# The key stage of an RWKV-7 layer in fp32: PE order by hand, head sums on quarters of the array, on-chip low-rank results, stores from ACT

## The chip, the cores and the metric

The kernel runs on one core of a Trainium2 chip. The metric is the device time of one launch in microseconds: the median of three runs. Engines are called PE (TensorE, matrix products; PEld is its weight load), DVE (VectorE), ACT (ScalarE), POOL (GpSimd) and SP (SyncE, which here only issues transfers). Each engine takes its own instructions strictly in order and waits on semaphores for the others.

## The reference

A decoder trunk with two layers over 272 tokens (16 learned tokens and 256 of the input) of 2048 features: an RWKV-7 time mixing, a gated linear attention, each followed by a squared-ReLU MLP. The change lies in the time mixing of the first layer. What matters of it:

```python
def rwkv7_time_mix(x, v_first, mix, w_rkv, w0, w1, w2, a0, a1, a2, g1, g2, k_k, k_a, r_k,
                   ln_w, ln_b, w_o, vres):
    xx = jnp.pad(x, ((0, 0), (1, 0), (0, 0)))[:, :-1] - x
    xr, xw, xk, xv, xa, xg = (x + xx * mix[i] for i in range(6))
    r = xr @ w_rkv[0]
    k = xk @ w_rkv[1]
    v = xv @ w_rkv[2]
...
    w_log = -jax.nn.softplus(-(w0 + jnp.tanh(xw @ w1) @ w2)) - 0.5
    a = jax.nn.sigmoid(a0 + (xa @ a1) @ a2)
    kk = hs(k * k_k)
    kk = kk / jnp.maximum(jnp.sqrt(jnp.sum(kk * kk, axis=-1, keepdims=True)), 1e-12)
    k = k * (1.0 + (a - 1.0) * k_a)
    decay = jnp.exp(-jnp.exp(hs(w_log)))
    y = rwkv7_scan(rh, decay, kh, vh, -kk, kk * ah)
...
    bonus = (jnp.sum(rh * kh * r_k, axis=-1, keepdims=True) * vh).reshape(B, T, D)
```

`hs` splits the 2048 features into 32 heads of 64. The scan is computed in chunks of 64 tokens: the products of decayed keys and queries, a triangular system for each head that is inverted, and a state step for each chunk.

## The kernel before

Features lie on the 128 partitions, tokens along the free dimension, so a tensor of the layer is 16 tiles of 128 x 272. A weight for one output tile comes in two halves of 512 KB. `wload` (line 128) loads a half with SP into `raw` (three buffers), ACT rounds it into `hi` (line 140), DVE subtracts into `lo` (line 141), both with two buffers; the PE then does 24 matmuls on it (`mm3`, lines 163 to 165: hi by x-high, hi by x-low, lo by x-high). A tile of a projection is thus 48 matmuls of 128 x 128 by 272.

The key stage (lines 567 to 618) runs over the 16 tiles f of the key projection. In each:

- `proj` gives k in a PSUM bank (`pj`, or `pry` for every third tile).
- `ca` holds the decay's cumulated sum and `a` of this tile. The low-rank function `lora` (lines 470 to 481) made them during the stage before, for all 16 tiles, and stored them to DRAM as `cad`; here they are loaded again. ACT turns the first into `W` and `iW` (L574, L575), one buffer for `W` and two for `iW`.
- ACT makes `kk` (L576), its square `sq` (L577) and `kn` (L578). The sum of `sq` within each head is a matmul of the full array with `bones`, a matrix of ones in two 64 x 64 blocks on the diagonal (L580). ACT makes an inverse root of it (L581, L582), DVE scales `kk` (L584).
- DVE fills two tiles of 128 x 576 with `put`: `bk` (the keys, L300 with `iW`) and `ar` (kk and r with `W`). Both have two buffers. SP stores them to DRAM as `bkd` and `ard` (L590, L593).
- DVE makes r times k times r_k in `kn` (L591), a second full matmul with `bones` sums it (L595), ACT copies that over `r` (L596).

Into the same loop are put: at f = 0 the blend of the value projection's input, `mix(3)`; at f = 7 the transfers that fetch the first eight tiles' `bk` and `ar` in another layout, 1 MB each (`fetch`, into `BK0` and `AR0`); at f = 10 to 13 the products of keys and queries (`scores`, PE L525, DVE `AM`); from f = 13 the steps of the inversion (`invert`, all on DVE). The value projection follows at once.

Each engine's order comes from a scheduler that follows the order of the program and moves instructions ahead where it reckons that they fit, with weight loads and casts at a higher priority; the order is fixed when the kernel is built. It puts a sum of tile f between two matmuls of tile f + 1. Only in the later part of the layer is the PE's order written out by hand (`tc.manual_schedule`).

Of the kernel before, what the change touches and what calls it, by code (L numbers as in the profile page):

```python
# [11 lines left out]
F32R = mybir.dt.float32r  # L12
AF = mybir.ActivationFunctionType
ALU = mybir.AluOpType
# [40 lines left out]
class Kern:  # L55
# [242 lines left out]
    def rwkv(self, done):  # L298
# [171 lines left out]
        def lora(f):  # L470
            l2 = self.t(e2, [96, 2, P], "l2", 3)
            nc.sync.dma_start(l2, ap["lora2"][f])
            st = self.t(ep, [P, 2, T], "ca", 2)
# [7 lines left out]
            nc.sync.dma_start(cad[f], st.rearrange("p a t -> p (a t)"))  # L481

        xg = mix32(5, ep)
        for f in range(NR + 2, KT):
            nc.scalar.copy(self.two(rr[f]), self.proj(pair(wr, f), xr, T))
            if f == NR + 2:
                for i in range(2):
                    nc.scalar.activation(gs[i], self.proj32(pair(lw, 2 + i), xg, T), AF.Sigmoid)
                xk = mix(2, ep)
            for i in range(3 if f < 14 else 2):  # L490
                lora(3 * (f - 10) + i if f < 14 else 12 + 2 * (f - 14) + i)
# [4 lines left out]
        Wf = self.t(ep, [P, T + 1], "W")  # L496
        nc.gpsimd.memset(Wf[:, 0:1], 1.0)
        W = Wf[:, 1:]
# [68 lines left out]
        for f in range(KT):  # L567
            r = rr[f]
            bk, ar = st2[0][f % 2], st2[1][f % 2]
            ps = self.proj(pair(wk, f), xk, T, bank=self.pry if f % 3 == 2 else None)  # L570
            ca = self.t(ep, [P, 2, T], "ca", 2)
            nc.sync.dma_start(ca.rearrange("p a t -> p (a t)"), cad[f])
            iW, kk, sq, kn = (self.t(ep, [P, T], n, 2) for n in ("iW", "kk", "sq", "kn"))
            nc.scalar.activation(W, ca[:, 0], AF.Exp, scale=-DECAY)  # L574
            nc.scalar.activation(iW, ca[:, 0], AF.Exp, scale=DECAY)  # L575
            nc.scalar.mul(self.two(kk), ps, self.vec("k_k", f))  # L576
            nc.scalar.activation(sq, kk, AF.Square)  # L577
            nc.scalar.activation(kn, ca[:, 1], AF.Identity, scale=self.vec("k_a", f), bias=self.omka[:, f : f + 1])  # L578
            ss = self.pm()[:, :T]
            nc.tensor.matmul(ss, self.bones, sq, start=True, stop=True)  # L580
# [3 lines left out]
            nc.vector.scalar_tensor_tensor(out=kk, in0=sq, scalar=1e12, in1=kk, op0=ALU.min, op1=ALU.mult)  # L584
            put(ar, 0, kk, Wf[:, :T], 1)
            nc.vector.tensor_copy(ar[:, 0:513:128], kk[:, ::C])
# [4 lines left out]
            nc.vector.scalar_tensor_tensor(out=kn, in0=r, scalar=self.vec("r_k", f), in1=kn, op0=ALU.mult, op1=ALU.mult)  # L591
            put(ar, 1, r, W)
            nc.sync.dma_start(ard[f], ar)  # L593
            rk = self.pu()[:, :T]
            nc.tensor.matmul(rk, self.bones, kn, start=True, stop=True)  # L595
            nc.scalar.copy(r, rk)  # L596
            nc.vector.tensor_copy(WC[:, f], W[:, C - 1 : 4 * C : C])
            if f == 0:
                xv = mix(3, self.xp)
                early2.close()  # L600
                wl = ExitStack()
                lp = wl.enter_context(tc.tile_pool(name="wl", bufs=1, reuse_waits="tile"))
                BKs, ARs = ([self.t(lp, [P, 8, 256], n)] for n in ("BK0", "AR0"))
                AMs, AMrs = [self.t(lp, [P, 2, 16, 128], "AM0")], []
                sysA = self.t(lp, [P, 32, 32], "sysA")
                t11 = sysA.rearrange("p a b -> p (a b)")[64:96].rearrange("p (c h s) -> p c h s", c=2, h=16)
                nc.gpsimd.memset(sysA, 0.0)
# [14 lines left out]
        BKs.append(self.t(kp, [P, 8, 320], "BK1"))  # L622
# [699 lines left out]
```

## Time and profile before

| | us |
|---|---|
| median of 3 runs | 2402.7 (2400.86 to 2403.1) |
| the profiled execution | 2402.54 |
| its span in the profile | 2400.8 |
| the key stage, 155.31 to 278.90 | 123.59 |

A row of the PE's timeline has the start in us, the duration in us, engine, line and operation, the tile written and the tiles read, the shapes and a count; a bracket at the end gives the idle time before it and who ended that. One fp32 matmul by `bones` leaves two records (x2), a fast one leaves one. In a group's row the two numbers after the bar are busy us and mean ns of one, and behind the second bar stands idle time before them.

### The profile page before, as it was taken

The page shows a single profiled execution, that of the slowest core. Times are in us where ns is not written, and L with a number is a line of the kernel's source. Part 1 is how long each engine was busy: PE and PEld are TensorE (multiplying, and loading weights), DVE is VectorE, ACT ScalarE, POOL GpSimd, SP SyncE. Part 2 cuts the span into 40 slices and gives each one's busy share as a digit, 9 for nine tenths or more (in the row PEclk, how much of TensorE's full clock was granted, in tenths as well). Part 3 has the DMA queues.
Part 4 walks back from the last instruction along what each step waited for, and adds up shares of the span by engine and source line. Part 5 has one row for each costly group of instructions (what it writes and reads, how often), then busy time and mean ns, then how long its engine had stood idle before and what let it go on. Part 6 is the DMA issues. An engine that isn't in the chain of part 4 may idle for free. (4 is left out here: it accounts for less than half of the span.)

```text
span 2400.8 us, 48047 instructions
## 1 busy us (share of the span) xinstructions
PE 2360.9 (98%) x19689; PEld 2244.1 (93%) x19689; DVE 1611.9 (67%) x2734; ACT 1242.4 (52%) x1975; POOL 6.6 (0%) x20
## 2 busy tenths in 40 slices
PE   9999999899999999999999999999999999999998
PEld 8888888889999999999999999999999999999997
DVE  8777886858655555555556777767666666666666
ACT  6376644556555445445345556555555445445444
POOL 0000000000000000000000000000000000000000
PEclk9999999999999999999999999999999999999999
DMA  6578864524555555555555554455555555555554
GB/s 210 169 235 293 248 190 146 146 83 163 183 187 193 187 191 191 188 193 186 192 189 190 196 181 167 159 176 193 182 201 200 200 201 200 202 202 202 201 201 169
DMA packets 160732, 455.34 MB, mean 190 GB/s; under 512 B 34112, under 2 KB 50624, under 8 KB 160512
## 3 DMA queue, kind: packets, MB, share of 16 engines
q1 hardware_dynamic: 160512, 452.27, 55.8%
q8 instruction: 154, 2.52, 0.4%
q14 instruction: 66, 0.54, 0.1%
HBM read 433.86 MB, written 18.35 MB: 188 GB/s over the span
## 5 line engine op out<-in xcount | busy, mean ns | idle before, releaser
L141 DVE TENSOR_TENSOR lo<-raw,hi 128x1024 fp32r<-128x1024 f32 (+1 forms) x818 | 927.4, 1140 | 534.1 <-ACT hi L140 525.9
L140 ACT CAST hi<-raw 128x1024 fp32r<-128x1024 f32 (+1 forms) x818 | 794.6, 979 | 939.4 <-PE pj L164 546.8
L163 PE MATMUL pj<-x,hi 128*128 128x272 f32 (+1 forms) x2624 | 748.6, 285 | 1.7 <-DVE hres L300 1.0
L165 PE MATMUL pj<-x,lo 128*128 128x272 f32 (+1 forms) x2624 | 734.5, 280 | 4.3 <-DVE lo L141 4.1
L164 PE MATMUL pj<-x,hi 128*128 128x272 f32 (+1 forms) x2624 | 734.0, 280 | 0.2 <-DVE x L240 0.2
L163 PEld LDWEIGHTS pj<-x,hi 128*128 128x128 f32 x2624 | 498.1, 190 | 10.2 <-issue 3.7
L165 PEld LDWEIGHTS pj<-x,lo 128*128 128x128 f32 x2624 | 498.2, 190 | 7.2 <-DVE lo L141 6.5
L164 PEld LDWEIGHTS pj<-x,hi 128*128 128x128 f32 x2624 | 498.2, 190 | 3.6 <-issue 1.4
L196 PE MATMUL pj<-x,hi 128*128 128x512 f32 x1280 | 419.9, 382 | 0.1
L197 PE MATMUL pj<-x,lo 128*128 128x256 f32 x1280 | 348.8, 273 | 0.0
L196 PE MATMUL pj<-h,hi 128*128 128x512 f32 x1008 | 330.3, 382 | 0.0
L163 PE MATMUL pj<-h,hi 128*128 128x272 f32 (+1 forms) x1040 | 290.1, 279 | 0.0
L164 PE MATMUL pj<-h,hi 128*128 128x272 f32 (+1 forms) x1040 | 290.1, 279 | 0.0
L165 PE MATMUL pj<-h,lo 128*128 128x272 f32 (+1 forms) x1040 | 290.1, 279 | 0.0
L197 PE MATMUL pj<-h,lo 128*128 128x256 f32 x1008 | 274.8, 273 | 0.0
L196 PEld LDWEIGHTS pj<-x,hi 128*128 128x128 f32 x1280 | 241.9, 189 | 34.1 <-DVE x L996 0.4
L197 PEld LDWEIGHTS pj<-x,lo 128*128 128x128 f32 x1280 | 245.7, 192 | 0.3 <-DVE lo L141 0.2
L196 PEld LDWEIGHTS pj<-h,hi 128*128 128x128 f32 x1008 | 190.5, 189 | 26.5
L163 PEld LDWEIGHTS pj<-h,hi 128*128 128x128 f32 x1040 | 196.6, 189 | 0.0
L164 PEld LDWEIGHTS pj<-h,hi 128*128 128x128 f32 x1040 | 196.6, 189 | 0.0
L165 PEld LDWEIGHTS pj<-h,lo 128*128 128x128 f32 x1040 | 196.6, 189 | 0.0
L197 PEld LDWEIGHTS pj<-h,lo 128*128 128x128 f32 x1008 | 193.5, 192 | 0.0
(270 smaller groups left out, 2077.2 us busy)
## 6 DMA issues: line engine op xcount, KB each, us to landing
raw<-mlp_w_d SPq DMA_DIRECT2D x512, 512.0 KB, 3.3
raw<-gla_in_d SPq DMA_DIRECT2D x98, 512.0 KB, 3.2
raw<-w_rkv_d SPq DMA_DIRECT2D x80, 512.0 KB, 3.9
raw<-gla_o_d SPq DMA_DIRECT2D x32, 512.0 KB, 4.3
raw<-w_r_d SPq DMA_DIRECT2D x16, 512.0 KB, 3.3
raw<-rw_oQ_d SPq DMA_DIRECT2D x16, 512.0 KB, 3.2
ard<-ar SPq DMA_DIRECT2D x16, 288.0 KB, 3.4
bkd<-bk SPq DMA_DIRECT2D x16, 288.0 KB, 3.5
```

The costliest lines, as they stand in the source:

```text
L140: nc.scalar.copy(hi[:, h], raw[:, h])
L141: nc.vector.tensor_tensor(out=lo[:, h], in0=raw[:, h], in1=hi[:, h].bitcast(F32), op=ALU.subtract)
L163: nc.tensor.matmul(out, hi[:, ws], xh, start=first, stop=False)
L164: nc.tensor.matmul(out, hi[:, ws], xl, start=False, stop=False)
L165: nc.tensor.matmul(out, lo[:, ws], xh, start=False, stop=last)
L196: nc.tensor.matmul(wide, hi[:, ws], xt, start=kt == 0, stop=False)
L197: nc.tensor.matmul(one, lo[:, ws], xt[:, 0], start=False, stop=kt == nk - 1)
```

## The change

Nothing else in the layer is computed differently. By parts:

- The PE's order in the key stage is written out by hand: half of tile f, `sums` of tile f - 1, the other half of tile f. `rest(f - 1)` stands between the halves in the program, too, and so shifts the place of all other engines' work.
- `sums` replaces both full matmuls with `bones` by four of 64 x 64: two on the array's diagonal quarters for `sq` (into `pm`), two on the other two quarters for the tile before's `kn` (into `pu`, with the two heads swapped; ACT copies them back crosswise, L595, in two copies of 64 partitions).
- `lora` keeps the results of tiles 0 to 7 in `hres` in SBUF and stores none of them. Those of tiles 8 to 15 are stored, and each is loaded into the place that tile f - 8 has left (L637).
- `W` has two buffers. r times W and k times iW are put before the inverse root's result is used. The five-column copy into `ar` and the copy into `WC` move from DVE to ACT (L632, L639).
- The stores of `bk` and `ar` are issued by ACT. In tiles 4 to 7 each is split in two, with one part going straight into `BK0`, `AR0` or `BK1`; tiles 0 to 3 are fetched into these by SP at f = 5, 6 and 7. `BK1` (the second keys) gets a place of its own from the start of the stage, and its later fetch goes.
- The blend for the value projection is made during the stage before, in place; only its rounding (`hl`) remains, at f = 1. `scores` and the inversion begin one tile earlier.

```diff
--- before.py
+++ after.py
@@ -470,7 +470,7 @@
         def lora(f):
             l2 = self.t(e2, [96, 2, P], "l2", 3)
             nc.sync.dma_start(l2, ap["lora2"][f])
-            st = self.t(ep, [P, 2, T], "ca", 2)
+            st = hres[:, 2 * f : 2 * f + 2] if f < NR else self.t(ep, [P, 2, T], "ca", 2)
...
             nc.vector.tensor_tensor_scan(out=st[:, 0], data0=m64, data1=sg, initial=0.0, op0=ALU.mult, op1=ALU.add)
-            nc.sync.dma_start(cad[f], st.rearrange("p a t -> p (a t)"))
+            if f >= NR:
+                nc.sync.dma_start(cad[f], st.rearrange("p a t -> p (a t)"))
...
                 xk = mix(2, ep)
+            if f == KT - 2:
+                for kt in range(KT):
+                    mixed(d[:, kt], kt, 3)
             for i in range(3 if f < 14 else 2):
                 lora(3 * (f - 10) + i if f < 14 else 12 + 2 * (f - 14) + i)
         tc.keep_in_program_order(nc.scalar.preload_act_table_set("natural_log_exp_and_others"))
         st2 = [[self.t(ep, [P, 576], n, 2) for i in range(2)] for n in ("bk", "ar")]
         for x in st2[0] + st2[1]:
             nc.gpsimd.memset(x[:, 512:], 0.0)
-        Wf = self.t(ep, [P, T + 1], "W")
-        nc.gpsimd.memset(Wf[:, 0:1], 1.0)
-        W = Wf[:, 1:]
+        Wfs = [self.t(ep, [P, T + 1], "W", 2) for _ in range(2)]
+        for x in Wfs:
+            nc.gpsimd.memset(x[:, 0:1], 1.0)
 
         def put(dst, slot, a, b, skip=0):
             v = dst[:, :512].rearrange("q (c s t) -> q c s t", c=4, s=2)[:, :, slot]
@@ -564,62 +568,114 @@
                 for rows, x in reversed(blocks(c, slice(0, 16))):
                     nc.sync.dma_start(x, invd[b][rows].rearrange("h s t -> s h t"))
 
-        for f in range(KT):
-            r = rr[f]
+        def store(f, dst, x, i):
+            q = nc.scalar
+            if 3 < f < 8:
+                q.dma_start((BKs, ARs)[i][0][:, f], x[:, :256])
+                q.dma_start(dst[f][:, 256:] if i else BKs[1][:, f], x[:, 256:])
+            else:
+                q.dma_start(dst[f], x)
+
+        held, tiles = [], {}
+
+        half = lambda q: slice(HEAD * q, HEAD * q + HEAD)
+
+        def sums(sq):
+            ss, last = self.pm()[:, :T] if sq is not None else None, held.pop() if held else None
+            todo = [(sq, ss, 0)] if sq is not None else []
+            if last:
+                r, kn = last
+                rk = self.pu()[:, :T]
+                todo.append((kn, rk, 1))
+            for x, out, i in todo:
+                for q in range(2):
+                    nc.tensor.matmul(out[half(q ^ i)], self.bones[half(q), half(q)], x[half(q)], start=True, stop=True)
+            if last:
+                for q in range(2):
+                    nc.scalar.copy(r[half(q)], rk[half(1 - q)])
+            return ss
+
+        def keyproj(f, ps, half):
+            hi, lo = self.wload(pair(wk, f)[half])
+            for j in range(8):
+                kt = 8 * half + j
+                self.mm3(ps, hi, lo, slice(j * P, (j + 1) * P), xk[kt][:, 0], xk[kt][:, 1], kt == 0, kt == KT - 1)
+
+        def front(f, ps):
+            kk, sq = (self.t(ep, [P, T], n, 2) for n in ("kk", "sq"))
+            ps = self.back(ps)
+            nc.scalar.mul(self.two(kk), ps, self.vec("k_k", f))
+            nc.scalar.activation(sq, kk, AF.Square)
+            tiles[f] = ps, kk, sq
+
+        def rest(f):
+            r, Wf = rr[f], Wfs[f % 2]
+            W = Wf[:, 1:]
             bk, ar = st2[0][f % 2], st2[1][f % 2]
-            ps = self.proj(pair(wk, f), xk, T, bank=self.pry if f % 3 == 2 else None)
-            ca = self.t(ep, [P, 2, T], "ca", 2)
-            nc.sync.dma_start(ca.rearrange("p a t -> p (a t)"), cad[f])
-            iW, kk, sq, kn = (self.t(ep, [P, T], n, 2) for n in ("iW", "kk", "sq", "kn"))
+            ps, kk, sq = tiles.pop(f)
+            i = f % NR
+            ca = hres[:, 2 * i : 2 * i + 2]
+            iW, kn = (self.t(ep, [P, T], n, 2) for n in ("iW", "kn"))
+            nc.scalar.activation(kn, ca[:, 1], AF.Identity, scale=self.vec("k_a", f), bias=self.omka[:, f : f + 1])
+            tt(self.two(kn), ps, self.two(kn))
+            ss = sums(sq)
             nc.scalar.activation(W, ca[:, 0], AF.Exp, scale=-DECAY)
             nc.scalar.activation(iW, ca[:, 0], AF.Exp, scale=DECAY)
-            nc.scalar.mul(self.two(kk), ps, self.vec("k_k", f))
-            nc.scalar.activation(sq, kk, AF.Square)
-            nc.scalar.activation(kn, ca[:, 1], AF.Identity, scale=self.vec("k_a", f), bias=self.omka[:, f : f + 1])
-            ss = self.pm()[:, :T]
-            nc.tensor.matmul(ss, self.bones, sq, start=True, stop=True)
             nc.scalar.activation(sq, ss, AF.Ln, bias=self.tiny)
             nc.scalar.activation(sq, sq, AF.Exp, scale=-0.5)
-            tt(self.two(kn), ps, self.two(kn))
+            put(bk, 0, kn, iW)
+            put(ar, 1, r, W)
+            nc.vector.scalar_tensor_tensor(out=kn, in0=r, scalar=self.vec("r_k", f), in1=kn, op0=ALU.mult, op1=ALU.mult)
+            held.append((r, kn))
             nc.vector.scalar_tensor_tensor(out=kk, in0=sq, scalar=1e12, in1=kk, op0=ALU.min, op1=ALU.mult)
             put(ar, 0, kk, Wf[:, :T], 1)
-            nc.vector.tensor_copy(ar[:, 0:513:128], kk[:, ::C])
+            nc.scalar.copy(ar[:, 0:513:128], kk[:, ::C])
+            store(f, ard, ar, 1)
             tt(kk, kk, ca[:, 1])
             put(bk, 1, kk, iW)
-            put(bk, 0, kn, iW)
-            nc.sync.dma_start(bkd[f], bk)
-            nc.vector.scalar_tensor_tensor(out=kn, in0=r, scalar=self.vec("r_k", f), in1=kn, op0=ALU.mult, op1=ALU.mult)
-            put(ar, 1, r, W)
-            nc.sync.dma_start(ard[f], ar)
-            rk = self.pu()[:, :T]
-            nc.tensor.matmul(rk, self.bones, kn, start=True, stop=True)
-            nc.scalar.copy(r, rk)
-            nc.vector.tensor_copy(WC[:, f], W[:, C - 1 : 4 * C : C])
-            if f == 0:
-                xv = mix(3, self.xp)
...
-            if f == 7:
-                fetch(0, BKs, bkd)
-                fetch(0, ARs, ard)
-            if 9 < f < 14:
-                scores(0, (f - 10) // 2, f % 2)
-            if f == 13:
-                inv = invert(0)
-            if f > 13:
-                for _ in range(6):
-                    next(inv, None)
+            if f < NR:
+                nc.sync.dma_start(ca.rearrange("p a t -> p (a t)"), cad[f + NR])
+            store(f, bkd, bk, 0)
+            nc.scalar.copy(WC[:, f], W[:, C - 1 : 4 * C : C])
+
+        with tc.manual_schedule(engines={ENG.PE}):
+            for f in range(KT + 1):
+                if f < KT:
+                    ps = (self.pry if f % 3 == 2 else self.pj)()[:, :T]
+                    keyproj(f, ps, 0)
+                if f:
+                    rest(f - 1)
+                if f < KT:
+                    keyproj(f, ps, 1)
+                    front(f, ps)
+                if f == 1:
+                    xv = [self.t(self.xp, [P, 2, T], "x", KT, F32R) for _ in range(KT)]
+                    for kt in range(KT):
+                        hl(xv[kt], d[:, kt])
...
+                    BKs.append(self.t(lp, [P, 8, 320], "BK1"))
...
+                if f in (5, 6, 7):
+                    dst, src, i, j = ((BKs[0], bkd, 0, 256), (ARs[0], ard, 0, 256), (BKs[1], bkd, 256, 576))[f - 5]
+                    nc.sync.dma_start(dst[:, :4], src[:4, :, i:j].rearrange("f p n -> p f n"))
+                if 8 < f < 13:
+                    scores(0, (f - 9) // 2, (f + 1) % 2)
+                if f == 12:
+                    inv = invert(0)
+                if f > 12:
+                    for _ in range(6):
+                        next(inv, None)
+            sums(None)
...
-        BKs.append(self.t(kp, [P, 8, 320], "BK1"))
@@ -892,7 +948,6 @@
         units1 = ((2, 0), (2, 1), (3, 0), (3, 1), (4, 0))
         self.split_parts = 2
         for i in ((0, 128), (128, 320)):
-            fetch(1, BKs, bkd, i)
             fetch(1, ARs, ard, i)
         ahead()
         with tc.manual_schedule(engines={mybir.EngineType.PE}):
```

Three places where the instructions' order differs. In the rows, a name's number tells buffers apart, and `waits` names the engine, or the DMA queue (DMAHW), whose semaphore the instruction waits for; a wait on its own engine guards a result still on its way.

DVE, up to a tile's `kk`. 1790 and 1791 are the two buffers of `ar`, `bk` likewise; `r_23` is r of tile 8, `r_24` and `r_25` are those of tiles 9 and 10. Before, tile 8 (the first row follows the `kk` of tile 7):

```order
L300 TENSOR_TENSOR ar_1790<-r_23_97,W_1796 128x4x64 [waits DMAHW7_49,Activation_49]
L300 TENSOR_TENSOR bk_1789<-kk_2616,iW_2615 128x4x64 [waits DVE_49]
L300 TENSOR_TENSOR bk_1789<-kk_2616,iW_2615 128x16
L300 TENSOR_TENSOR ar_1790<-r_23_97,W_1796 128x16
L597 COPY WC_105<-W_1796 128x4
L141 TENSOR_TENSOR lo_2778<-raw_2775,hi_2777 128x1024 [waits DMAHW0_49,PE_49,Activation_49]
L300 TENSOR_TENSOR kn_2715<-pry_2649,kn_2715 128x272 [waits Activation_49]
L300 TENSOR_TENSOR bk_1788<-kn_2715,iW_2712 128x4x64 [waits DMAHW1_49,DVE_49]
L300 TENSOR_TENSOR bk_1788<-kn_2715,iW_2712 128x16
L591 SCALAR_TENSOR_TENSOR kn_2715<-r_23_97,vecs_126,kn_2715 128x272 [waits DVE_49]
L584 SCALAR_TENSOR_TENSOR kk_2713<-sq_2714,kk_2713 128x272 [waits Activation_49]
L300 TENSOR_TENSOR ar_1790<-kk_2713,W_1796 128x4x64 [waits DVE_49]
```

After, from behind the `kk` of tile 8 to that of tile 9:

```order
L300 TENSOR_TENSOR kn_2849<-pj_2707,kn_2849 128x272 [waits Activation_49]
L300 TENSOR_TENSOR ar_1790<-r_25_99,W_1796 128x4x64 [waits DMAHW3_49]
L300 TENSOR_TENSOR bk_1789<-kn_2849,iW_2848 128x4x64 [waits DMAHW7_49,DMAHW0_49,DVE_49]
L300 TENSOR_TENSOR bk_1789<-kn_2849,iW_2848 128x16
L300 TENSOR_TENSOR ar_1790<-r_25_99,W_1796 128x16
L628 SCALAR_TENSOR_TENSOR kn_2849<-r_24_98,vecs_126,kn_2849 128x272 [waits DVE_49]
L141 TENSOR_TENSOR lo_2931<-raw_2928,hi_2930 128x1024 [waits DMAHW1_49,PE_49,Activation_49]
L630 SCALAR_TENSOR_TENSOR kk_2799<-sq_2800,kk_2799 128x272 [waits Activation_49]
L300 TENSOR_TENSOR ar_1791<-kk_2799,W_1797 128x4x64 [waits DVE_49]
L300 TENSOR_TENSOR ar_1791<-kk_2799,W_1797 128x15
```

The product of r and W for a tile (`ar<-r`) used to stand behind the `kk` of the tile before, and so a whole tile after the buffer's last store was issued. Now the product of tile 10 stands ahead of the `kk` of tile 9, behind that of tile 8, and waits for the DMA that stores tile 8's `ar` from the same buffer.

ACT, at a tile's `kk` and `sq`, where the next weight cast (`hi`) stands. Before:

```order
L140 CAST hi_2300<-raw_2298 128x1024 [waits DMAHW6_49,PE_49]
L575 ACTIVATE iW_2235<-ca_2233 128x272
L576 ACTIVATE kk_2236<-pj_2172,vecs_126 128x272 [waits PE_49]
L578 ACTIVATE kn_2238<-ca_2233,om_k_a_206,vecs_126 128x272
L577 ACTIVATE sq_2237<-kk_2236 128x272 [waits Activation_49]
L140 CAST hi_2365<-raw_2363 128x1024 [waits DMAHW0_49,PE_49]
L581 ACTIVATE sq_2237<-pm_2244,tiny_128 128x272 [waits PE_49]
L582 ACTIVATE sq_2237<-sq_2237 128x272 [waits Activation_49]
```

After (tile 1):

```order
L632 COPY ar_1790<-kk_1863 128x5 [waits DVE_49,Pool_49]
L622 ACTIVATE W_1796<-hres_72 128x272 [waits DVE_49]
L577 DMA ard_80<-ar_1790 128x576 [waits Activation_49]
L140 CAST hi_2082<-raw_2080 128x1024 [waits DMAHW5_49,PE_49]
L577 DMA bkd_79<-bk_1788 128x576 [waits DVE_49]
L607 ACTIVATE kk_1955<-pj_1867,vecs_126 128x272 [waits PE_49]
L140 CAST hi_2117<-raw_2115 128x1024 [waits DMAHW6_49,PE_49]
L608 ACTIVATE sq_1956<-kk_1955 128x272 [waits Activation_49]
L623 ACTIVATE iW_2145<-hres_72 128x272
L639 COPY WC_105<-W_1796 128x4
L624 ACTIVATE sq_1956<-pm_2052,tiny_128 128x272 [waits PE_49,Activation_49]
```

Here the cast, which waits for the PE to free a weight buffer, has moved between `kk` and `sq`; the logarithm of the summed `sq` (L624) stands behind it. The order is of this kind in tiles 1, 3, 5, 7 and 13, and `sq` stands ahead of the cast in the others. The store of `ar` follows the five-column copy, the store of `bk` follows the cast before.

PE, at a sum. Before:

```order
L163 MATMUL pj_2457<-x_1209,hi_2460 128x272
L164 MATMUL pj_2457<-x_1209,hi_2460 128x272
L165 MATMUL pj_2457<-x_1209,lo_2461 128x272
L580 MATMUL pm_2434<-sq_2427,cst_125 128x272 [waits Activation_49]
L163 MATMUL pj_2457<-x_1210,hi_2460 128x272
L164 MATMUL pj_2457<-x_1210,hi_2460 128x272
L165 MATMUL pj_2457<-x_1210,lo_2461 128x272
```

After:

```order
L163 MATMUL pj_2508<-x_1212,hi_2511 128x272
L164 MATMUL pj_2508<-x_1212,hi_2511 128x272
L165 MATMUL pj_2508<-x_1212,lo_2512 128x272
L592 MATMUL pm_2543<-sq_2504,cst_125 64x272 [waits PE_49,Activation_49]
L592 MATMUL pm_2543<-sq_2504,cst_125 64x272
L592 MATMUL pu_2544<-kn_2440,cst_125 64x272 [waits DVE_49]
L592 MATMUL pu_2544<-kn_2440,cst_125 64x272
L163 MATMUL pj_2508<-x_1213,hi_2575 128x272
L164 MATMUL pj_2508<-x_1213,hi_2575 128x272
```

Single sums that stood within a half, one for `sq` and, elsewhere in the tile, one for `kn`, have become one group of four between two halves.

More of the change, by code (lines that the diff above doesn't have):

```diff
@@ L597, in rwkv @@
-            nc.vector.tensor_copy(WC[:, f], W[:, C - 1 : 4 * C : C])
-            if f == 0:
-                xv = mix(3, self.xp)
[L600 to L607, printed above, removed]
@@ new lines, in rwkv @@
+        with tc.manual_schedule(engines={ENG.PE}):
[12 more added lines that the diff above has]
+                        hl(xv[kt], d[:, kt])
+                    early2.close()
+                    wl = ExitStack()
+                    lp = wl.enter_context(tc.tile_pool(name="wl", bufs=1, reuse_waits="tile"))
+                    BKs, ARs = ([self.t(lp, [P, 8, 256], n)] for n in ("BK0", "AR0"))
+                    BKs.append(self.t(lp, [P, 8, 320], "BK1"))
+                    AMs, AMrs = [self.t(lp, [P, 2, 16, 128], "AM0")], []
+                    sysA = self.t(lp, [P, 32, 32], "sysA")
+                    t11 = sysA.rearrange("p a b -> p (a b)")[64:96].rearrange("p (c h s) -> p c h s", c=2, h=16)
+                    nc.gpsimd.memset(sysA, 0.0)
+                if f in (5, 6, 7):
[9 more added lines that the diff above has]
+            sums(None)
```

## The prediction

> **What bounds the kernel now.** I read the page's first parts and the chain of waits, then the windows of the key stage, then the PE's timeline and waits inside it. TensorE is busy 98% of the span at full clock, and the chain that ended last holds no engine but PE.
>
> ```profile
> PE 2360.9 (98%) x19689; PEld 2244.1 (93%) x19689; DVE 1611.9 (67%) x2734; ACT 1242.4 (52%) x1975; POOL 6.6 (0%) x20
> ...
> PEclk9999999999999999999999999999999999999999
> ...
> PE 28%; DVE 0%; ACT 0%; DVEq 0%; issue 0%
> 155.31:278.90 123.59, 117.08 (x900) 108.71 (x899) 105.29 (x275) 86.41 (x170) 1.11 (x2) 1.00 0.82 267
> 278.90:301.47 22.57, 20.82 (x172) 20.14 (x171) 21.32 (x62) 11.79 (x26) 0.00 (x0) 1.00 0.81 265
> ```
>
> The two window rows (length; then PE, PEld, DVE, ACT, POOL; clock, DMA share, GB/s) are the key stage, from its first matmul to its last, and the start of the v-projection. In the key stage the PE is still the fullest engine (117 of 123.6 us), but DVE has 105, ACT 86, and the DMA engines are 82% busy. What can be won is PE's extra work and its waits; what can be lost is a wait on any of the others.
>
> ```profile
> 154.59 0.62 PE L475 MATMUL pm<-tw,l 96*128 96x272 f32 x2
> 155.05 0.62 PE L476 MATMUL pry<-ta,l 96*128 96x272 f32 x2
> ...
> 201.04 0.72 PE L580 MATMUL pm<-sq,cst 128*128 128x272 f32 x2
> ...
> 201.72 0.28 PE L164 MATMUL pj<-x,hi 128*128 128x272 f32 x1
> ...
> 207.62 0.28 PE L165 MATMUL pj<-x,lo 128*128 128x272 f32 x1
> 208.03 0.73 PE L580 MATMUL pm<-sq,cst 128*128 128x272 f32 x2
> ...
> 288.26 0.28 PE L164 MATMUL pj<-x,hi 128*128 128x272 f32 x1
> ...
> 301.24 0.28 PE L165 MATMUL pj<-x,lo 128*128 128x272 f32 x1
> PE pm L580 <- ACT sq L577: 3.8, 5, 1.7
> PE pu L595 <- DVE kn L591: 2.0, 3, 1.7
> PE pt L525 <- DMA BK<-bkd: 1.4, 1, 1.4
> ```
>
> One tile is the time between two `L580`: 208.03 − 201.04 = 7.0 us. From 288.26 to 301.24 the PE runs 113 fast matmuls in a row, 112 steps of 0.116 us, so the 48 of a tile take 5.55. The low-rank pair shows one fp32 matmul at full size: 155.05 − 154.59 = 0.46 us (its two records are its two passes). From 201.72 to 207.62 there are 46 fast steps (5.33) and one `L595`, so an inserted sum costs 0.57: 0.46 and 0.11 of changing over. Two of them, and a wait of about 0.3 for `sq`, make up the 7.0. The three waits rows (155 to 300 us; total, times, longest) hold 7.2 us in all.
>
> **The change, part by part.** *PE order and sums.* A tile becomes 24 matmuls, four quarter matmuls, 24 matmuls. If all four quarters run at once they take 0.57 with the changeover, if two by two 2 × 0.46 + 0.11 = 1.03, if one by one 4 × 0.46 + 0.11 = 1.95. The nearest rows are the 64×64 matmuls of the state steps:
>
> ```profile
> L720 PE MATMUL pry<-AR,S 64*64 64x64 f32 x32 | 1.6, 231 | 0.0
> L722 PE MATMUL pu<-S,AR 64*64 64x64 f32 x32 | 1.2, 221 | 0.0
> 353.75 0.27 PE L722 MATMUL pu<-S,AR 64*64 64x64 f32 x1
> ```
>
> Their 64 records begin at 353.75 and end within the window's 355.2, about 1.45 us. One by one a record of 64 columns would take 0.46 / 2 × 64 / 272 = 0.054, together 3.46 us. So 2.4 ran at once, pipeline fill included. I take 0.75 and keep 0.57 and 1.95. A tile then costs the PE 5.55 + 0.75 = 6.3 us where nothing waits.
>
> The Trainium skill, page "TensorEngine Tiling (Array Packing)", section "Gotcha 1: PSUM Pressure", says that different row tiles cannot access the same PSUM bank simultaneously; both `sq` quarters write `pm` and lie in different row tiles. By it the quarters go two by two at best and the time would be 2398.2 by the sum below. The 2.4 of the state rows, whose row tiles also share a bank, speaks against a strict form of it.
>
> *ACT order.* In tiles 1, 3, 5, 7 and 13 the changed ACT order sets a weight cast, which waits for the PE to finish the half before, ahead of `sq` (the second order listing above). The cast and `sq` then delay the sums by their lengths, 1.04 + 0.43, about 1.45 us. Five such tiles: +7.25. If another wait holds the PE anyway, this hides in it.
>
> ```profile
> L140 ACT CAST hi<-raw 128x1024 fp32r<-128x1024 f32 x16 | 16.7, 1044 | 6.7 <-PE pj L164 5.0 <-PE pry L164 1.7
> L577 ACT ACTIVATE sq<-kk 128x272 f32<-128x272 f32 x8 | 3.4, 429 | 0.2
> ```
>
> *Scores.* Four inserts of `L525` as before, 1.2 us each, one tile earlier (4.8 in all); the 1.4 us wait for `BK` goes, since half of it is copied inside the chip and the rest fetched in three parts.
>
> *The ar loop.* The product `r·W` of tile f+2 now stands on DVE ahead of the `kk` of tile f+1, and must wait until the store of tile f's `ar`, two buffers back, has landed (the first order listing). Before, it stood behind the `kk` of tile f+1, a whole tile after that store was issued. Queued behind it are `bk`, `kn`, a weight's `lo` part, and then tile f+1's own `kk`, whose store the next round waits for. So a round of DVE and DMA closes on itself, whatever PE does:
>
> ```profile
> 217.03 0.44 DVE L584 SCALAR_TENSOR_TENSOR kk<-sq,kk 128x272 f32<-128x272 f32 x1
> 217.51 0.51 DVE L300 TENSOR_TENSOR ar<-kk,W 128x256 f32<-128x256 f32 x2
> 217.97 0.17 DVE L586 COPY ar<-kk 128x5 f32<-128x5 f32 x1
> 218.07 1.23 DVE L141 TENSOR_TENSOR lo<-raw,hi 128x1024 fp32r<-128x1024 f32 x1
> 219.22 0.43 DVE L300 TENSOR_TENSOR kk<-kk,ca 128x272 f32<-128x272 f32 x1
> 219.57 0.42 DVE L300 TENSOR_TENSOR ar<-r,W 128x256 f32<-128x256 f32 x1
> 219.91 0.50 DVE L300 TENSOR_TENSOR bk<-kk,iW 128x256 f32<-128x256 f32 x2
> 220.33 0.17 DVE L300 TENSOR_TENSOR ar<-r,W 128x16 f32<-128x16 f32 x1
> 220.41 0.16 DVE L597 COPY WC<-W 128x4 f32<-128x4 f32 x1
> ...
> 223.56 0.50 DVE L591 SCALAR_TENSOR_TENSOR kn<-r,vecs,kn 128x272 f32<-128x272 f32 x1
> 224.02 0.44 DVE L584 SCALAR_TENSOR_TENSOR kk<-sq,kk 128x272 f32<-128x272 f32 x1
> DMA to landing us min/median/max: 2.2/3.4/5.5
> raw<-w_rkv_d SPq DMA_DIRECT2D x35, 512.0 KB, 4.2
> ```
>
> From start to start: `kk` 0.48, its put 0.46, the five-column copy on ACT some 0.26 with its semaphores, so the store is issued 1.2 after `kk` begins. It lands after L. Then 0.05, `ar<-r` 0.34, `bk` 0.42, the last columns 0.08, `L591` 0.46, `lo` 1.15: 2.5. A round is 3.7 + L. In tiles 0 and 2 `kn` stands inside it too (0.46 by the step 223.56 to 224.02 of an operation of that size), in tiles 1 and 3 `kn` and a second `lo` (+1.6), in tile 12 `kn` and four steps of the inversion (+1.25; a step at 0.2, an estimate from the small rows above). Tile 13 is filled with inversion steps, 7.1 by adding the same rows and sixteen steps.
>
> The trace has no DMA issued by ACT. L is bounded below by the fastest `ard` store, 2.2, and above by the loads' 4.2, which such a store could come to share; the median of the same 288 KB is 3.4. On ACT's own queue the store no longer stands behind SP's loads, and 2.2 MB of `ca` loads (of 33 MB at 267 GB/s) leave the stage. I take the middle of minimum and median, 2.8.
>
> The Trainium skill, page "DMA: Bandwidth & Descriptors", section "Issuing engines are not separate DMA queues", says that issuing from several engines saves only the issuing time, since all run on the same 16 DMA engines. By it L stays 3.4. No row of this trace can show which.
>
> *The sum of the key stage.* The first sums come 9.35 us after its start (48 + 24 matmuls 8.33, one low-rank pair 0.92, 0.1 of gaps); then 14 rounds; then 0.75 + 2.78 to its end. At L = 2.8: tiles 0 and 2 2 × 6.96, tiles 1 and 3 2 × 8.1, tiles 4 to 7 by PE (6.3 and 7.75 in turn) 28.1, tiles 8 to 11 by PE with scores 4 × 7.5, tile 12 7.75, tile 13 7.1: 103.1. End at 116.0 against 123.6 before: −7.6.
>
> *Behind it.* The sums of tile 15 already wait 1.75 us among the v-projection's matmuls:
>
> ```profile
> 281.37 0.28 PE L165 MATMUL pj<-x,lo 128*128 128x272 f32 x1
> 283.39 0.72 PE L580 MATMUL pm<-sq,cst 128*128 128x272 f32 x2 [1.75 <-ACT sq L577]
> ...
> 313.72 0.38 PE L165 MATMUL pj<-x,lo 128*128 128x272 f32 x1 [1.03 <-DVE lo L141]
> ...
> 326.33 0.38 PE L165 MATMUL pj<-x,lo 128*128 128x272 f32 x1 [1.03 <-DVE lo L141]
> ```
>
> Now ACT's `kk` of tile 15 stands behind a copy that waits for DVE, and DVE has a `lo` (1.15) in front: +1.35. The last `kn` sum, alone, adds 0.45. Quarters for full matmuls save 0.1. The two waits of 1.03 for `lo` should shrink, since inversion starts a tile earlier: −0.8. Together +0.9.
>
> *Costed at nothing.* The sixteen blends moved ahead of the stage (DVE is free a third of the span, and no PE wait above lies there; uncovered, 16 operations of the size of `L591`, 0.5 us each, would be 8 us); the copies and issues moved to ACT, below 0.5 us each by the ACT rows, hidden while ACT (86 of 123.6 us) waits for PE; without that cover they put up to 1 us a tile on the ACT order above. Fewer SP issues free a queue that bounds nothing.
>
> **Rivals.** (1) *The stores land as before*, L = 3.4: rounds 7.56, 8.7, 7.1, 7.5 (PE), 8.35, 7.1 sum to 106.4, end 119.3, −4.3 + 0.9: 2399.1. For it: same bytes, DMA 82% busy; against: the freed queue. (2) *The loop never closes*, L near 2.2 or less of a chain than I read: PE alone, 14 × 6.3 + 7.25 + 4.8 = 100.3, end 113.2, −10.4 + 0.9: 2393.0. (3) *Slower: ACT's stores share the engines evenly with the 512 KB loads* and land like them, 4.2: rounds 8.36, 9.5, 7.9, 7.9, 9.15, 7.9 sum to 116.0, end 128.9, +5.3 + 0.9: 2408.7. It decides from L = 3.75 (no gain) and passes +0.2% at 4.1. For it: 82% DMA share; four issues a tile in tiles 4 to 7. Against: 3.4 now, behind SP's loads. (4) *The quarters do not overlap*: 14 × 7.5 + 7.25 + 4.8 = 117, end 131.1: 2410.9. Against: the state rows.
>
> **How the numbers follow.** All sums stand against the profiled execution, 2402.54 us with a span of 2400.8; the median 2402.7 is the same within 0.2. Forecast: 2402.5 − 7.6 + 0.9 = 2395.8, say 2396, chance 0.35. Rivals: (1) 0.18, (2) 0.25, (3) 0.17, (4) 0.05. The likeliest one's own range, L from 2.5 to 3.1 and sums from 0.6 to 0.9, is 2394 to 2398. The 8-in-10 range must hold (1), (2) and most of (3): 2389 (case 2 with half of the ACT waits hidden) to 2408. A run here can tell 0.2%, 4.8 us, from no change. Faster by more: most of the forecast 0.29, all of (2), a little of (1): 0.58. Within: the rest of these and a part of (3): 0.23. Slower: 0.19.
>
> **What would show it.** Between the halves of a tile, from the last fast matmul to the next, about 0.75 us where nothing waits; over 1 says two by two, near 2 rival (4). Sums that wait some 1.4 us on `sq` in tiles 1, 3, 5, 7, 13. `ar<-r` on DVE held by a DMA in most tiles from 0 to 7, and `ard` landing some 2.8 us after its issue; no such idle time says rival (2), over 4 us rival (3). The key stage some 116 us long; a wait near 3.1 before tile 15's sums. The forecast is wrong if DVE's idle time there comes from ACT, not from a store, or if ACT falls behind its casts so that `lo` holds the PE.

## The result, and the profile after

| | before | changed |
|---|---|---|
| median, us | 2402.06 (2399.43 to 2405.4, 14 runs) | 2406.38 (2404.42 to 2413.38, 14 runs) |
| ratio, 95% interval | | 1.0022 (1.0015 to 1.0029) |
| profiled execution, us | 2402.54 | 2408.51 |
| its span, us | 2400.8 | 2406.7 |

The change makes the kernel slower by 0.22%. The forecast was 2396 us; the time lies inside the range of 2389 to 2408, close to rival (3), and on the other side of "before".

The page's engine row and the queue of ACT's transfers (packets, MB, share), then the two windows that answer to those shown of before (length; PE, PEld, DVE, ACT, POOL; clock, DMA share, GB/s):

```profile
PE 2355.9 (98%) x19753; PEld 2236.7 (93%) x19753; DVE 1608.9 (67%) x2702; ACT 1257.9 (52%) x2027; POOL 6.7 (0%) x21
...
q10 hardware_dynamic: 5760, 9.44, 1.1%
```

```profile
155.41:288.66 133.25, 113.00 (x954) 101.88 (x953) 101.82 (x243) 92.68 (x202) 1.10 (x2) 0.97 0.69 229
288.66:310.58 21.92, 21.32 (x182) 19.96 (x181) 21.04 (x57) 12.41 (x28) 0.00 (x0) 1.00 0.72 236
```

The PE has 5 us less to do in the whole kernel, as intended, and the key stage is nevertheless 133.25 us long, to the first matmul of the value projection, where it was 123.4 to the same matmul (155.31 to 278.71). The DMA share fell from 0.82 to 0.69, so over the whole stage the transfers had more room than before (in single stretches it still reaches 0.93). The time is in waits. The waits of the stage (155 to 288 us; total, times, longest):

```profile
ACT ar L632 <- DVE ar L300: 19.9, 14, 2.4
PE pm L592 <- ACT sq L608: 18.3, 10, 2.8
DVE ar L300 <- DMA ard<-ar: 16.3, 8, 3.1
...
ACT hi L140 <- DVE bk L300: 3.6, 3, 1.4
```

Before, PE's waits from 155 to 300 us were 7.2 us. Now the sums alone wait 18.3 us for `sq`, DVE waits 16.3 us for stores, and ACT 19.9 us in front of its new five-column copy. PE's timeline shows where (the first records of the `sq` quarters in tiles 1 to 8, 10 and 11, and their wait):

```profile
173.38 0.45 PE L592 MATMUL pm<-sq,cst 64*64 64x272 f32 x2 [1.35 <-ACT sq L608]
181.46 0.45 PE L592 MATMUL pm<-sq,cst 64*64 64x272 f32 x2 [1.63 <-ACT sq L608]
189.94 0.45 PE L592 MATMUL pm<-sq,cst 64*64 64x272 f32 x2 [1.51 <-ACT sq L608]
198.56 0.45 PE L592 MATMUL pm<-sq,cst 64*64 64x272 f32 x2 [1.72 <-ACT sq L608]
208.60 0.45 PE L592 MATMUL pm<-sq,cst 64*64 64x272 f32 x2 [2.26 <-ACT sq L608]
218.03 0.45 PE L592 MATMUL pm<-sq,cst 64*64 64x272 f32 x2 [1.32 <-ACT sq L608]
226.57 0.45 PE L592 MATMUL pm<-sq,cst 64*64 64x272 f32 x2 [2.10 <-ACT sq L608]
234.86 0.45 PE L592 MATMUL pm<-sq,cst 64*64 64x272 f32 x2 [1.84 <-ACT sq L608]
...
250.19 0.45 PE L592 MATMUL pm<-sq,cst 64*64 64x272 f32 x2
257.86 0.45 PE L592 MATMUL pm<-sq,cst 64*64 64x272 f32 x2
```

Every tile from 1 to 8 waits, not every second one. In tiles 9 to 12 the `scores` matmuls lengthen PE's own round to 7.66 us (257.86 − 250.19), and there are no waits; tiles 13 and 14 wait again, 1.72 and 2.83 us. So a round of some 8 to 10 us, not the PE, sets tiles 1 to 8. One such round, from the timelines of DVE and ACT (in order of time within each engine; the first ACT row is the issue of a store):

```profile
199.12 0.43 DVE L300 TENSOR_TENSOR ar<-r,W 128x256 f32<-128x256 f32 x1 [3.09 <-DMA ard<-ar]
199.47 1.22 DVE L141 TENSOR_TENSOR lo<-raw,hi 128x1024 fp32r<-128x1024 f32 x1
...
202.04 1.22 DVE L141 TENSOR_TENSOR lo<-raw,hi 128x1024 fp32r<-128x1024 f32 x1
203.17 0.44 DVE L630 SCALAR_TENSOR_TENSOR kk<-sq,kk 128x272 f32<-128x272 f32 x1
```

```profile
195.04 0.33 ACTq L577 DMA_DIRECT2D ard<-ar  x1
...
200.74 0.43 ACT L625 ACTIVATE sq<-sq 128x272 f32<-128x272 f32 x1
...
204.10 0.20 ACT L632 COPY ar<-kk 128x5 f32<-128x5 f32 x1 [2.43 <-DVE ar L300]
...
204.89 1.05 ACT L140 CAST hi<-raw 128x1024 fp32r<-128x1024 f32 x1 [0.26 <-ACT W L622]
...
206.80 0.49 ACT L607 ACTIVATE kk<-pry,vecs 128x272 f32<-128x272 f32 x1 [0.86 <-PE pj L165]
207.18 1.03 ACT L140 CAST hi<-raw 128x1024 fp32r<-128x1024 f32 x1
208.12 0.43 ACT L608 ACTIVATE sq<-kk 128x272 f32<-128x272 f32 x1
```

DVE stops 3.09 us at the product of r and W for the store that was issued 4 us earlier, at 195.04. Two `lo` parts and `kk` queue behind it, and DVE works without a pause from 199.12 to `kk` at 203.17. ACT reaches the five-column copy and stops 2.43 us, since `kk` is late; the next weight cast is queued behind the copy, the PE's next half behind the cast, the next `kk` on ACT behind that half (0.86), and `sq` behind one more cast. The PE then waits 2.26 us at its sums. So ACT and PE are late because DVE is. They do not hold DVE in return: the inverse root that `kk` needs was ready at 201.17 (L625), 2 us before DVE came to it, and ACT stood waiting with the copy that goes ahead of the next store. That store is late by the landing of the one before and by DVE's queue, not by ACT or PE.

### The profile page after: what moved, and what is told of

Same layout as the page of the kernel before. It is cut to its first block, busy times and chain, and to the rows that moved or that the text cites. A ratio compares the mean times of both kernels' runs of the same rounds, so it can differ in the third digit from the quotient of the medians.

```text
span 2406.7 us, 48185 instructions
## 1 busy us (share of the span) xinstructions
PE 2355.9 (98%) x19753; PEld 2236.7 (93%) x19753; DVE 1608.9 (67%) x2702; ACT 1257.9 (52%) x2027; POOL 6.7 (0%) x21
```

## Experiments

All times are medians, with the ratio to the kernel before on the same chip. Two suspected causes are taken apart: **A**, the place of the r·W product on DVE, in front of the next `kk` and behind a store just issued; **B**, the order on ACT, where in tiles 1, 3, 5, 7 and 13 a weight cast stands between `kk` and `sq`.

### e1: a third buffer for ar

```diff
-            st = hres[:, 2 * f : 2 * f + 2] if f < NR else self.t(ep, [P, 2, T], "ca", 2)
+            st = hres[:, 2 * f : 2 * f + 2] if f < NR else self.t(ep, [P, 576], "ca", 2)[:, : 2 * T].rearrange("p (a t) -> p a t", a=2)
...
+        st2[1].append(self.t(ep, [P, 576], "ca", 2))
...
-            bk, ar = st2[0][f % 2], st2[1][f % 2]
+            bk, ar = st2[0][f % 2], st2[1][f % 3]
```

> A third buffer for ar (one of the slots of ca, which nothing else uses any more). Theory A (the loop through the store of ar): the product of r and W no longer waits for a store issued a moment before, DVE's 16.3 us of waits on the ard DMA fall under 2 us, the key stage falls from 131.5 us to 114-118, and the total by 8 to 14 us, to 2392-2399. Theory B (the order on ACT, a weight cast ahead of sq, holds the PE, and DVE's wait is idle time that costs nothing): the order on ACT is unchanged, so the waits for sq and the total stay within 3 us of the changed kernel's. Theory C (the stores' and fetches' traffic slows the weight loads): no change either.

2399.7 us (2397.14 to 2401.15, 10 runs), ratio 0.9987 (0.9977 to 0.9996): 6.7 us under the changed kernel. DVE's wait for the stores is gone from the list, but the sums still wait:

```profile
PE pm L593 <- ACT sq L609: 12.9, 9, 3.1
```

The total missed A's range by little, the stage clearly: 124.4 us, not 114 to 118. So A alone is not the whole of it, and B, which said no change, is not either.

### e2: the stores issued by SP

```diff
-            q = nc.scalar
+            q = nc.sync
```

> The stores are issued by SP again, everything else as in the changed kernel. The scheduler then puts sq ahead of the cast in every tile of the key stage, while the product of r and W still stands between one tile's kk and the next one's. Theory A: the loop through the store stays; if the stores land as they did from SP before (3.4 us median) the total falls by no more than 5 us. Theory B: the waits for sq vanish and the total falls by 7 us or more. If ACT's queue itself made the stores land late, the landing falls from 3.9 to about 3.4 us.

2398.0 us (2395.05 to 2402.47, 10 runs), ratio 0.9978 (0.9966 to 0.999). With ACT rid of the issues, the scheduler puts `sq` ahead of the cast in every tile. It moves DVE's work as well: in tiles 0 to 3 the changed kernel has the r·W product ahead of `kn`, in tiles 1 and 3 ahead of both `lo` parts; here it stands behind `kn` and one `lo` in all of them, and from its start to `kk` it is 2.0 to 2.4 us instead of 2.9 and 4.1. So this run takes away B and part of A. The waits halve and do not vanish:

```profile
PE pm L592 <- ACT sq L608: 9.0, 10, 3.6
DVE ar L300 <- DMA ard<-ar: 8.1, 9, 1.9
```

8.4 us are won, more than A allowed and as much as B asked for, while both waits are still there. Neither theory alone fits. In tiles 0 to 3 the `ar` stores landed 4.1, 3.3, 4.9 and 3.3 us after their issue from SP, and 4.8, 3.2, 4.5 and 4.0 from ACT in the changed kernel, so the issuing engine matters little.

### e3: both

The edits of e1 and e2 together.

> Third ar buffer and stores by SP. Theory A with the ACT order as the second term: PE alone sets the stage, 112-114 us, total 2388-2393, several us under e1. Theory B: the same as e2.

2388.1 us (2387.1 to 2391.92, 4 runs), ratio 0.9935 (0.9912 to 0.9959). 18.3 us under the changed kernel, where the two parts alone took 6.7 and 8.4: both together give 3.2 us more than their sum, which is within the scatter of these four runs. The stage is 113.6 us long.

### e4: sums on the full array

```diff
-                for q in range(2):
-                    nc.tensor.matmul(out[half(q ^ i)], self.bones[half(q), half(q)], x[half(q)], start=True, stop=True)
+                nc.tensor.matmul(out, self.bones, x, start=True, stop=True)
             if last:
-                for q in range(2):
-                    nc.scalar.copy(r[half(q)], rk[half(1 - q)])
+                nc.scalar.copy(r, rk)
```

> The four quarter matmuls of a tile are two matmuls of the full array again (2 x 0.46 us), in the same place of the PE's order. Theory A: in tiles 0 to 8 the loop hides the difference, and only tiles 9 to 12 and the last ones pay some 0.4 us each, +1 to +3 us. If the PE is the bound in all tiles: +6 to +8 us.

2410.7 us (2406.44 to 2413.29, 10 runs), ratio 1.0031 (1.002 to 1.0041): 4.3 us above the changed kernel, between the two expectations. Where nothing waits, a tile with `scores` takes 7.77 us for 7.67, so PE's own cost is 0.1 a tile. Most of the rest stands in tiles 4 to 7, where DVE's four rounds from `kk` to `kk` lengthen from 34.6 to 37.6 us: the r·W product has moved there, too, ahead of `kn` in tiles 5 to 7, and now waits for its store in all four rounds, before in two. The run is thus no clean price of the sums.

### e5: e1 with the square first

```diff
-            nc.scalar.mul(self.two(kk), ps, self.vec("k_k", f))
-            nc.scalar.activation(sq, kk, AF.Square)
+            nc.scalar.activation(self.two(sq), ps, AF.Square, scale=self.vec("k_k", f))
+            nc.scalar.mul(self.two(kk), ps, self.vec("k_k", f))
```

> e1 (third ar buffer, stores still by ACT), and sq is made straight from the PSUM bank, ahead of kk and not from kk, so that it stands ahead of the weight cast in every tile. If the order on ACT is what e1 still pays against e3, the total comes near e3's 2388 (2386-2391). If issuing the stores from ACT costs time by itself (issues that last longer or wait for earlier transfers, and hold ACT's casts), it stays near e1's 2399.7, at 2394 or more.

2390.9 us (2390.32 to 2392.27, 4 runs), ratio 0.9948 (0.9933 to 0.9964): 8.8 us under e1, with the stores still on ACT. So most of what e3 gains over e1 comes from the order on ACT. Whether issuing from ACT costs the remaining 2.8 us by itself these runs cannot tell, since the ranges of e3 and e5 overlap.

### e6 and e7: more off the stage

e6 is e3 with the square first; e7 is e3 with the five-column copy on DVE:

```diff
-            nc.scalar.copy(ar[:, 0:513:128], kk[:, ::C])
+            nc.vector.tensor_copy(ar[:, 0:513:128], kk[:, ::C])
```

> e3 (third ar buffer, stores by SP) with sq straight from the PSUM bank ahead of kk. In e3 the sums wait 6.1 us in five places of the stage (mostly the last tiles). sq comes 0.4 us earlier in every tile: 0 to -3 us against e3, 2385-2388.

> e3 with the five-column copy into ar on DVE again, so that ACT no longer stops in the middle of a tile to wait for DVE (in e3 16 us of idle time before that copy). If this stop holds ACT's casts, -1 to -4 us against e3; if ACT's idle time there costs nothing, within 1 us of e3.

2390.5 us (2384.38 to 2392.5, 4 runs; ratio 0.9942, 0.9921 to 0.9962) and 2388.7 us (2383.85 to 2390.71, 4 runs; 0.9936, 0.9913 to 0.9959): no gain over e3 that can be measured, though the stage became 2.2 and 1.1 us shorter in the profiled executions. In e3, where DVE is hardly late, the copy on ACT costs nothing; no run takes it back from the changed kernel itself.

### e8: the square first, nothing else

> The changed kernel (two ar buffers, stores by ACT) with sq straight from the PSUM bank ahead of kk: the order on ACT alone. The loop through the store stays, but DVE's order moves too: the product of r and W stands behind a weight's lo part in most tiles. If the two causes add up, 2398-2401; if the loop hides the order on ACT, 2404-2407.

2392.8 us (2391.07 to 2396.24, 5 runs), ratio 0.9956 (0.9943 to 0.997): better than expected, 13.6 us from two lines. The scheduler moved the r·W product behind a `lo` in most tiles as well, so this run takes away B and part of A; the stores' wait on DVE is down to 7.1 us, and little of it reaches the PE:

```profile
DVE ar L300 <- DMA ard<-ar: 7.1, 5, 1.9
PE pm L592 <- ACT sq L607: 2.2, 2, 2.0
```

### e9: one buffer for W

This takes away A alone, by undoing the one part of the change that let the product move. The order on ACT and the issues stay.

```diff
-        Wfs = [self.t(ep, [P, T + 1], "W", 2) for _ in range(2)]
+        Wfs = [self.t(ep, [P, T + 1], "W")]
...
-            r, Wf = rr[f], Wfs[f % 2]
+            r, Wf = rr[f], Wfs[0]
```

> The changed kernel with one buffer for W again, nothing else undone. The product of r and W for a tile then has to stand behind the kk put of the tile before, as in the kernel before, and no longer in front of the next kk and lo; the order on ACT keeps the cast ahead of sq in every other tile, and the stores stay on ACT. Theory A+B (two causes that add up): the waits of DVE for the ard store fall from 16 us to under 4, the alternating waits for sq of 1.4-1.7 us stay, total 2396-2401, like e1. If the double W buffer has no part in it, 2404 or more.

2398.9 us (2396.81 to 2400.84, 11 runs), ratio 0.9986 (0.9977 to 0.9995), in the expected range and beside e1. No row of DVE waiting for an `ard` store is left in the stage. PE's timeline now shows B by itself:

```profile
187.57 0.45 PE L592 MATMUL pm<-sq,cst 64*64 64x272 f32 x2 [1.35 <-ACT sq L608]
...
194.57 0.45 PE L592 MATMUL pm<-sq,cst 64*64 64x272 f32 x2 [0.55 <-ACT sq L608]
```

A tile with the cast ahead of `sq` waits 1.35 us, and the next one, with the good order, still 0.55.

### e10: e3 with sums on the full array

> e3 (PE sets the stage) with the full-array sums instead of the quarters, in the same place. e4 against the changed kernel shows 7.77 against 7.67 us in tiles where nothing waits, 0.1 us a tile. Quarters worth 0.1 a tile: +1 to +3 us against e3. Quarters worth the 0.3 a tile that my sum had (1.03 against 0.75): +4 to +6.

2386.7 us (2383.43 to 2388.48, 5 runs), ratio 0.9934 (0.9921 to 0.9946), below e3 by 1.4 us, with overlapping ranges: lower than either expectation. Here the PE sets the rounds, and a tile takes 6.48 us with full sums and 6.38 with quarters (first two rows: e10; last two: quarters in e11). The quarters save 0.1 us a tile, 1.6 in all, and the totals do not show it.

```profile
170.68 0.62 PE L592 MATMUL pm<-sq,cst 128*128 128x272 f32 x2
177.16 0.62 PE L592 MATMUL pm<-sq,cst 128*128 128x272 f32 x2
...
177.46 0.45 PE L593 MATMUL pm<-sq,cst 64*64 64x272 f32 x2
183.84 0.45 PE L593 MATMUL pm<-sq,cst 64*64 64x272 f32 x2
```

### e11: all of it; e12: one W and the stores by SP

e11 is e3 with the edits of e5 and e7. e12 is e9 and e2 together, two undone parts and no third buffer.

> Third ar buffer, stores by SP, five-column copy on DVE, sq first. No wait in the stage but PE's own work; e6 and e7 each took up to 2 us off e3's stage (111.5 and 112.6 against 113.6 us): 2384-2389.

> One W buffer and the stores by SP: both causes taken away without a third ar buffer. If the two causes are the placing of the r and W product and the order on ACT, the total is near e3's 2388 (2386-2392); if the third buffer does something of its own, 2394 or more.

e11: 2388.1 us (2384.62 to 2389.46, 5 runs), ratio 0.9937 (0.9925 to 0.995), with a stage of 108.6 us, the shortest; the median is e3's all the same, so these 5 us do not show in the total. e12: 2388.0 us (2386.16 to 2389.95, 5 runs), ratio 0.994 (0.9926 to 0.9953). The window of e12's stage, its waits and its stores of tiles 4 to 7:

```profile
155.48:266.72 111.24, 108.13 (x954) 98.18 (x953) 98.70 (x234) 91.80 (x202) 1.10 (x2) 1.00 0.81 272
```

```profile
PE pm L592 <- ACT sq L608: 2.7, 3, 1.5
...
DVE ar L300 <- DMA ard<-ar: 1.1, 1, 1.1
```

```profile
ard<-ar SPq DMA_DIRECT2D x4, 160.0 KB, 6.0
```

The stores of tiles 4 to 7 land after 6.0 us at the median, against 4.2 in the changed kernel, and only one of them is waited for, 1.1 us. How long a store takes counts only where work that is due stands behind the instruction that waits for it. e12 beats both kernels by undoing two parts of the change: it is 14 us under the one before, 18 under the changed one.

| r·W product \ order on ACT | cast ahead of `sq` | `sq` first |
|---|---|---|
| ahead of the next `kk` | 2406.4 (the change) | 2398.0 (e2; nearer to `kk` in tiles 0 to 3) |
| a tile later, or a third buffer | 2398.9 (e9), 2399.7 (e1) | 2388.0 (e12), 2388.1 (e3), 2390.9 (e5) |

The upper right field is not A alone, and no run has B taken away with DVE's order left as it was. The eight rounds from the `kk` of tile 0 to that of tile 8 on DVE take, in the profiled executions, 69.9 us in the changed kernel, 61.6 in e9, where B is left, 61.3 in e2 and 53.3 in e12.

## Why the prediction was wrong, by its steps

**The PE's rounds: right in kind.** A free tile of 48 matmuls and the sums takes 6.38 us; the sum had 6.3. The quarters' group costs 0.82 for 0.75. In the row of 242.53 us both `sq` quarters begin, with the `kn` quarters 0.01 us later, and their second records follow 0.28 us after:

```profile
242.53 0.45 PE L592 MATMUL pm<-sq,cst 64*64 64x272 f32 x2
242.54 0.45 PE L592 MATMUL pu<-kn,cst 64*64 64x272 f32 x2
242.81 0.40 PE L592 MATMUL pm<-sq,cst 64*64 64x272 f32 x2
242.82 0.40 PE L592 MATMUL pu<-kn,cst 64*64 64x272 f32 x2
```

All four run at once. The rule of the Trainium skill, page "TensorEngine Tiling (Array Packing)", section "Gotcha 1: PSUM Pressure", that different row tiles cannot use one PSUM bank at the same time, is not borne out by these rows: the two `sq` quarters write one bank. What the sum missed is that full matmuls in the same place cost only 0.93 (6.48 − 5.55, e10). Grouping the sums saved 0.2 of the 1.14 us a tile, the quarters 0.1. Two smaller terms were too short: the first sums came 10.19 us after the stage's start for 9.35, and from tile 14's sums to the end it was 5.28 us for 3.53, 1.7 of it lost to a lower clock (last section).

**The ar loop: seen, and sized too small. This is the step that failed.** The prediction had the loop as 3.7 + L with L = 2.8, the middle between minimum and median of the old stores. DVE's rows of the first rounds after (`kk`, then the r·W product that waits; the last two rows of this kind are in the round above):

```profile
167.81 0.43 DVE L630 SCALAR_TENSOR_TENSOR kk<-sq,kk 128x272 f32<-128x272 f32 x1
173.82 0.43 DVE L300 TENSOR_TENSOR ar<-r,W 128x256 f32<-128x256 f32 x1 [2.04 <-DMA ard<-ar]
176.73 0.43 DVE L630 SCALAR_TENSOR_TENSOR kk<-sq,kk 128x272 f32<-128x272 f32 x1
181.22 0.43 DVE L300 TENSOR_TENSOR ar<-r,W 128x256 f32<-128x256 f32 x1 [2.28 <-DMA ard<-ar]
185.27 0.44 DVE L630 SCALAR_TENSOR_TENSOR kk<-sq,kk 128x272 f32<-128x272 f32 x1
190.97 0.43 DVE L300 TENSOR_TENSOR ar<-r,W 128x256 f32<-128x256 f32 x1 [1.82 <-DMA ard<-ar]
193.89 0.43 DVE L630 SCALAR_TENSOR_TENSOR kk<-sq,kk 128x272 f32<-128x272 f32 x1
```

| tile of the store | landed, us | 3.7 + L and what else stands in the round | measured, `kk` to `kk` |
|---|---|---|---|
| 0 | 4.8 | 9.0 | 8.92 |
| 1 | 3.2 | 8.5 | 8.54 |
| 2 | 4.5 | 8.7 | 8.62 |
| 3 | 4.0 | 9.3 | 9.28 |
| 4 | 6.2 | 9.9 | 9.77 |
| 6 | 5.2 | 8.9 | 8.94 |

(What else stands in the round is the prediction's 0.46 in tiles 0 and 2 and 1.6 in tiles 1 and 3. In tiles 4 and 6 the store is issued in two pieces, the second 0.5 to 0.6 us behind the first, and L is from the first issue to the second landing.) The formula holds to 0.15 us in every round in which DVE waits among the first eight; L was wrong. It was 4.1 us on average in tiles 0 to 3, not 2.8, and above 5 in tiles 4 and 6, which the sum had given to the PE at 6.3 us each. The prediction left out that the second piece of a split store starts late. What made the stores land late is not settled: the same four of the kernel before landed 3.4, 2.5, 4.0 and 4.1 us after their issue, and those from SP in e2 as late as those from ACT. By the Trainium skill, page "DMA: Bandwidth & Descriptors", section "Issuing engines are not separate DMA queues", the transfers of all issuing engines run on the same 16 DMA engines. The landings of e2 agree with that.

Rival (3) had L = 4.2 and the nearer rounds. That its 2408.7 meets the profiled execution's 2408.5 is luck: its key stage gets 5.3 us longer and what follows 0.9 longer, measured are 9.9 longer and 3.6 shorter.

**The order on ACT: seen, sized a little low, and hidden in tiles 1 and 3 as the sum had it.** Five tiles at 1.45 us were added for the PE-bound case; the forecast's sum kept them in tiles 5 and 7 and took them as hidden in the loop in tiles 1, 3 and 13. The size was right (1.35) but left out the 0.55 us of the tile behind. The table above leaves nothing for it in tiles 0 to 4 and 6: there DVE's loop alone makes up the round. In tiles 5 and 7, where DVE does not wait for a store, the rounds are 7.97 and 7.89 us for the sum's 7.75. So A and B are not two costs that add up tile by tile in the changed kernel: in most of the first eight rounds A is the limit and B lies behind it. B's cost comes out when A is gone: the eight rounds are 61.6 us in e9 and 53.3 in e12. For tile 13 the runs do not separate the two.

**Costed at nothing: the copy and the issues on ACT.** The copy ties ACT to DVE in the middle of a tile; ACT stands 19.9 us in front of it. Taken back alone from e3 (e7) it gains nothing, which fits a carrier of DVE's lateness rather than a cost of its own. The issue of a `bk` store waits for DVE in the same way (3.6 us in front of casts). The blends moved ahead show no cost there: the stage begins at 155.41 us for 155.31.

**Behind the stage: +0.9 forecast, −3.6 measured.** Matching matmuls, the changed kernel is 9.9 us late where the value projection begins and 6.3 at the end. Tile 15's sums do not wait; the long wait is tile 14's, 2.83. The last `kn` sum costs 1.27 us, 0.51 of it a wait, for 0.45 forecast. One of the two waits for `lo` is gone, as forecast.

**What stays open.** No run puts the low-rank results back through DRAM, so the worth of keeping them in SBUF was not measured. Why the stores landed later than before is open. The 2.8 us between e3 and e5 and the 4.3 us of e4 are not explained to the end.

## What to carry to other kernels

A second buffer lets a scheduler move a product ahead, and so can move a wait for a transfer ahead of work that is due: after such a change look at what now stands behind each instruction that waits for a DMA. Size such a loop by the landings of the very stores in it, not by the middle of a kernel's range. Two engines that hand work to each other within a tile pass lateness on; a small copy or a store's issue moved to a "free" engine makes it wait for its neighbour, and casts queued behind it reach TensorE. When one limit hides another, take each away alone and both together before pricing either, and look whether the edit has moved another engine's order as well.

## What the runs showed of the hardware that was not expected

A wait of the PE can cost more than its length. The granted clock fell to half for 3.4 us twice in the changed kernel's stage, right behind its two longest waits (2.26 us until 208.60, 2.83 us until 283.38); waits up to 2.10 us there had no such effect. The length of a single wait does not decide alone: in e7 one of 1.76 us until 262.20 was followed by some 3.4 us at half clock (0.72 granted from 262 to 268 us), in e4 one of 2.53 us until 228.43 by none (1.00 from 227 to 235). The window behind the first (columns as above; the clock is the number before the DMA share):

```profile
209.00:218.00 9.00, 7.71 (x56) 7.29 (x48) 5.35 (x13) 4.92 (x13) 0.00 (x0) 0.81 0.93 322
```

Matmuls follow each other there every 0.227 us instead of 0.116 for 3.4 us (1 − 0.81 of the window's 9.00 us, 1.7 us, is lost to the clock, which at half clock takes 3.4), so each such stretch adds up to 1.7 us; at most 3.4 of the stage's 9.9 us are this. In e1 a wait of 3.08 us until 221.78 came with some 6.8 us at half clock:

```profile
221.00:228.00 7.00, 6.22 (x32) 5.41 (x33) 4.03 (x12) 3.52 (x10) 0.00 (x0) 0.53 0.67 213
```

The Trainium skill, page "TensorE: Matmul & The Clock Gate", section "Part 1: The HAM clock gate (the "warmup" mystery)", has the half rate and the 3.4 us unit, which these rows bear out, but puts the idle time that brings it on at a window of about 3.4 us; here 2.26 us was enough, and in e7 1.76.
